# An encoder layer on one core: the squares of the attention heads' outputs, summed in float32r halves instead of float32

## The chip, the core and the metric

The kernel runs on one core of a Trainium2 chip. Its time is the device time of one execution in microseconds (us). Before the change three runs gave 1216.11, 1216.69 and 1217.87 us, so the median is 1216.69 us. The profiled execution took 1216.07 us, and its span, from the first recorded instruction to the last, is 1214.2 us.

## What is computed

Two inputs x of 1024 x 1024 float32 (called g = 0 and g = 1) go through one encoder layer with shared weights. Cut to what matters here:

```
proj = layer_norm(x) @ w_in                 # 3584 columns
o    = (softmax(q1 k1) - lam * softmax(q2 k2)) @ v        # 4 heads, 128 wide
o_da = rms_norm(o, subln_g) * (1 - lam_init) * silu(g_da) # rms over the 128 columns of a head
o_cv = b * conv3(c * h) * silu(g_cv)
o_mx = memory_attention(q_mx, mem) * silu(g_mx)           # 256 memory tokens
y    = layer_norm(ALPHA * x + concat(o_da, o_cv, o_mx) @ w_o)

rms_norm(x, g) = x * rsqrt(mean(square(x)) + 1e-5) * g
```

The change touches the mean of squares inside `rms_norm` alone.

## The kernel before

Everything that feeds a large matrix product is kept as two float32r numbers, a high half and a low half whose sum is the float32 value. A product is then three float32r passes (high x high, high x low, low x high). The helper `hi_of` makes a high half on GpSimd (POOL), and `lo_of` makes the low half by a subtraction, on VectorE (DVE) unless another engine is named. In the profile all of these stand on the helpers' lines, L157 for `hi_of` and L160 for `lo_of`.

The program is a list of jobs: for each input and each of its 4 attention heads (and one memory attention) two halves of 512 query rows. There are thus 16 attention head halves, called head 1 to head 16 below in order of time (the four heads of g = 0 with two halves each, then those of g = 1). A job computes scores (`score`, L678), softmax (L685 the row maximum on DVE, L686 the exponential on ScalarE, ACT), the difference of the two softmaxes (L694 on DVE), transposes of the result on TensorE (PE, `turn`, L736), halves of these (`th` on ACT, `tl` on DVE) and products with v (`av`, L764 to L766, into `po`). Between these steps stand "fillers", eight steps of three 512-column passes for one 128 x 512 tile of the projections (L435 to L437), and at the end the passes of the output projection (L927).

No scheduler reorders anything: the order on each engine is the order in which the program emits instructions. A planner, `Flow`, counts modelled nanoseconds of PE work. `after(ns, fn)` emits `fn` once the count has gone on by `ns`, and `extra` is a list of short PE jobs, each with a due count, of which `run_extra` emits one when it is due, between two filler steps. Every engine works through its queue in order, so an instruction that waits holds all that stand behind it.

At the end of a head half, `end_head` squares `po` on ACT into `sq` (L788), scales `po` by gain and gate on DVE into `og` (L790), and puts `rms` on the `extra` list with a due count 5000 later. `rms` sums the squares over the 128 partitions: each of four 128 x 128 blocks of `sq` is the stationary operand and a column of ones the moving one (L796), so the sums come out with one query row per partition. They go to DVE (`ms`, L798), four small steps on POOL (L800 to L803), a transpose (L810), and by way of memory into `og` (L822).

Small intermediate tiles share a pool of five 128 x 512 buffers, called `ev`; a new tile takes a free buffer and its first writer waits for the last user of the old tile.

Of the kernel before, what the change touches and what calls it, by code (L numbers as in the profile page):

```python
# [27 lines left out]
F32 = mybir.dt.float32  # L28
F32R = mybir.dt.float32r
# [6 lines left out]
P = 128  # L36
D = 1024
S = 1024
HS = 512
# [60 lines left out]
class Flow:  # L100
# [10 lines left out]
    def after(self, ns, fn):  # L111

        done = []

        def once():
            if not done:
                done.append(True)
                fn()
        self.n += 1
        heapq.heappush(self.due, (self.t + ns, self.n, once))  # L120
        return once
# [8 lines left out]
def encoder(ctx, tc, x0, x1, xt1, memt, wt, wo, cols, lam4, rope, ln_rows, y0, y1):  # L130
# [3 lines left out]
    after = fl.after  # L134

    ctx.enter_context(tc.manual_schedule())
    pool = ctx.enter_context(tc.tile_pool(name="sb", bufs=1))
# [8 lines left out]
    def sb(shape, dt, tag, name):  # L146
        return pool.tile(shape, dt, tag=tag, name=name, bufs=BUFS.get(tag, 1))

    def bank(shape, name):

        return psX.tile(shape, F32, tag="x", name=name)

    dma = nc.sync.dma_start
    V, G, A, T = nc.vector, nc.gpsimd, nc.scalar, nc.tensor

    def hi_of(out, x, scale=1.0):
        G.tensor_scalar(out, x, scale, 1.0, op0=ALU.mult, op1=ALU.mult)  # L157

    def lo_of(out, x, hi, eng=None):
        (eng or V).tensor_tensor(out, x, hi.bitcast(F32), op=ALU.subtract)  # L160

    def flat(t, offset, ap):
        return bass.AP(tensor=t.tensor, offset=t.offset + offset, ap=ap)


    const = {}

    def constants():
        ident = const["ident"] = pool.tile([P, P], F32, name="ident")
        make_identity(nc, ident)  # L170
        ones = const["ones"] = pool.tile([P, 1], F32, name="ones")
        G.memset(ones, 1.0)
        mhalf = const["mhalf"] = pool.tile([P, 8], F32, name="mhalf")
        G.memset(mhalf, -0.5)
        ccol = const["ccol"] = pool.tile([P, 32], F32, name="ccol")
        dma(ccol, cols)
        lamt = const["lamt"] = sb([P, 4, DH], F32, "gt", "lamt")
        dma(lamt, flat(lam4, 0, [[0, P], [DH, 4], [1, DH]]))
        const["rope"] = pool.tile([P, 2, S], F32, name="ropet")
# [281 lines left out]
    def store(dst, src, ns=1500):  # L461
        after(ns, lambda: dma(dst, src))
# [165 lines left out]
    class Job:  # L628
# [156 lines left out]
        def end_head(self):  # L785
            po = self.po
            self.sq = sb([P, HS], F32, "sq", "sq")
            A.activation(self.sq, po, AF.Square)  # L788
            self.og = sb([P, HS], F32, "og", "og")
            V.scalar_tensor_tensor(self.og, po, const["gain"], self.gt[0], op0=ALU.mult, op1=ALU.mult)  # L790
            extra.append((fl.t + 5000, self.rms))

        def rms(self):
            pr = bank([P, 4], "pr")
            for i in range(4):
                T.matmul(pr[:, i:i + 1], self.sq[:, i * P:(i + 1) * P], const["ones"], start=True, stop=True)  # L796
            ms, r0 = sb([P, 4], F32, "small", "ms"), self.r0
            V.scalar_tensor_tensor(ms, pr, 1.0 / P, r0, op0=ALU.mult, op1=ALU.mult)  # L798
            rs = sb([P, 4], F32, "small", "rs")
            G.tensor_tensor(ms, ms, r0, op=ALU.mult)  # L800
            G.tensor_scalar(ms, ms, 1.0, EPS, op0=ALU.mult, op1=ALU.add)
            G.tensor_tensor(ms, ms, const["mhalf"][:, 0:4], op=ALU.pow)
            G.tensor_tensor(rs, ms, r0, op=ALU.mult)  # L803
            g, h, half, og = self.g, self.h, self.half, self.og
            rd = dram.tile([4, P], F32, name=f"rd{g}_{h}_{half}")

            def rows():

                pw = bank([4, P], "pw")
                T.transpose(pw, rs, const["ident"])  # L810
                rw = sb([4, P], F32, "sq", "rw")
                V.tensor_copy(rw, pw)
                fl.pe(110)
                after(2500, lambda: dma(rd, rw))
                after(9000, lambda: spread())

                def spread():
                    self.rb = sb([P, HS], F32, "sq", "rb")
                    dma(self.rb, flat(rd, 0, [[0, P], [1, HS]]))

                def fin():
                    G.tensor_tensor(og, og, self.rb, op=ALU.mult)  # L822
                    store(mix_d[g][half][h], og)
                after(13500, fin)
            extra.append((fl.t + 6000, rows))
            fl.pe(100)
# [204 lines left out]
    weights_load(("MV", 0))  # L1031
    load_x(0)
    constants()
    load_x(1)
    for kb in range(KB):
# [84 lines left out]
```

## Time and profile before

| | busy us | share of the span | instructions |
|---|---|---|---|
| PE, matmuls | 1175.9 | 97% | 5881 |
| PE, weight loads (PEld) | 922.0 | 76% | 5881 |
| DVE | 803.0 | 66% | 1156 |
| ACT | 426.2 | 35% | 703 |
| POOL | 415.7 | 34% | 466 |

The profiled execution took 1216.07 us with a span of 1214.2 us, so 1.9 us lie outside the span. Weight loads overlap matmuls, and the end of a matmul is modelled, so the busy share of PE says that it nearly always has work, not that it runs at its peak. The pitch of PE, the time between the starts of two matmuls that follow each other, is the better measure of what one costs. The start times below are microseconds from the start of the span.

### The profile page before, as it was taken

How to read it: one execution, taken by the hardware profiler on the slowest of the kernel's cores; microseconds unless marked ns; L12 is line 12 of the kernel's file. 1: busy time of each engine (PE TensorE's matmuls, PEld its weight loads, DVE VectorE, ACT ScalarE, POOL GpSimd, SP SyncE). 2: the span in 40 equal slices, each digit the busy share in tenths (PEclk: the TensorE clock that was granted, in tenths of full speed). 3: DMA queues.
4: the chain of work that ended last, by engine and by line, in shares of the span. 5: the costliest groups of instructions: out<-in, count | busy, mean ns of one | idle time of the engine just before them, and what ended most of it. 6: DMA issues, size and time to landing. Idle time of an engine off the chain costs nothing.

```text
span 1214.2 us, 15653 instructions
## 1 busy us (share of the span) xinstructions
PE 1175.9 (97%) x5881; PEld 922.0 (76%) x5881; DVE 803.0 (66%) x1156; ACT 426.2 (35%) x703; POOL 415.7 (34%) x466
## 2 busy tenths in 40 slices
PE   8899999999999999999999999999999998899997
PEld 6677777777777777788777777777777877788885
DVE  4779857666677675543766765665655456887776
ACT  4624333334233334334344333433433344111220
POOL 4754423352234430322311113023110346445443
PEclk9999999999999999999999999999999999999999
DMA  8366336433644389753321212312322368354341
GB/s 325 102 230 217 145 130 208 153 144 113 216 156 156 122 281 309 260 191 128 133 71 64 92 40 95 100 68 92 111 78 74 127 222 294 99 196 144 133 145 52
DMA packets 83644, 182.61 MB, mean 150 GB/s; under 512 B 7713, under 2 KB 26353, under 8 KB 83441
## 3 DMA queue, kind: packets, MB, share of 16 engines
q1 hardware_dynamic: 80112, 175.33, 41.3%
q10 hardware_dynamic: 3456, 6.29, 1.3%
q8 instruction: 46, 0.75, 0.3%
q14 instruction: 30, 0.24, 0.1%
HBM read 119.69 MB, written 61.91 MB: 150 GB/s over the span
## 4 chain that ended last, share of the span: by engine, by line
PE 75%; DVE 11%; POOL 3%; issue 3%; ACT 3%; DMA 3%; SPq 0%; POOLq 0%; DVEq 0%; ACTq 0%
PE pout L927 13%; PE ps L678 7%; PE pt L736 5%; PE po L764 3%; PE pG L435 2%; PE po L766 2%; PE po L765 2%; PE pG L437 2%; PE pG L436 2%; DVE mx L685 2%; PE pQ L435 2%; PE pQ L437 2%; PE pQ L436 2%; ACT e L686 2%; PE pV L435 2%
## 5 line engine op out<-in xcount | busy, mean ns | idle before, releaser
L686 ACT ACTIVATE e<-ps,mx 128x1024 f32<-128x1024 f32 x128 | 142.8, 1116 | 295.8 <-DVE mx L685 295.6
L685 DVE TENSOR_REDUCE mx<-ps 128x1 f32<-128x1024 f32 x128 | 150.6, 1218 | 87.7 <-PE ps L678 87.7
L160 DVE TENSOR_TENSOR tl<-pt,th 128x1024 fp32r<-128x1024 f32 x80 | 97.3, 1217 | 11.7 <-ACT th L742 11.6
L927 PE MATMUL pout<-woh,mixh 128*128 128x512 f32 x256 | 100.6, 393 | 0.0
L927 PE MATMUL pout<-woh,mixl 128*128 128x512 f32 x256 | 100.4, 392 | 0.0
L927 PE MATMUL pout<-wol,mixh 128*128 128x512 f32 x256 | 100.2, 391 | 0.0
L742 ACT ACTIVATE th<-pt 128x1024 fp32r<-128x1024 f32 x80 | 82.3, 1029 | 42.6 <-PE pt L736 42.1
L694 DVE SCALAR_TENSOR_TENSOR e<-e,ssum,e 128x1024 f32<-128x1024 f32 x64 | 87.9, 1373 | 0.0
L919 POOL TENSOR_TENSOR xr<-xr,lnrow 128x512 f32<-128x512 f32 x32 | 55.7, 1758 | 68.9 <-DVE xr L916 68.8
L476 POOL TENSOR_TENSOR sw<-sw,ropet 128x512 f32<-128x512 f32 x32 | 41.7, 1302 | 90.7 <-DVE sw L470 88.1
L736 PE MATMUL pt<-ident,e 128*128 128x128 f32 x512 | 66.8, 274 | 4.8 <-ACT e L686 4.8
L736 PEld LDWEIGHTS pt<-ident,e 128*128 128x128 f32 x512 | 58.9, 141 | 16.1 <-ACT e L686 8.1
L678 PE MATMUL ps<-kh,qh 64*128 64x512 f32 x256 | 62.8, 444 | 5.4 <-DVE tl L160 5.4
L722 POOL TENSOR_SCALAR em<-em,rm 128x256 f32<-128x256 f32 x64 | 31.9, 517 | 83.2 <-DVE rm L720 76.4
L160 DVE TENSOR_TENSOR wl<-wraw,wh 128x1024 fp32r<-128x1024 f32 (+1 forms) x33 | 43.0, 1303 | 23.7 <-POOL wh L157 13.8
L908 ACT ACTIVATE mixh<-mraw 128x1024 fp32r<-128x1024 f32 x16 | 17.0, 1061 | 114.6 <-PE pout L927 97.6
L764 PE MATMUL po<-th,vh 128*128 128x512 f32 x128 | 56.7, 443 | 0.0
L927 PEld LDWEIGHTS pout<-woh,mixl 128*128 128x128 f32 x256 | 48.3, 189 | 10.8 <-DVE mixl L160 0.6
L678 PE MATMUL ps<-kl,qh 64*128 64x512 f32 x256 | 54.6, 392 | 1.6 <-DVE kl L479 1.5
L927 PEld LDWEIGHTS pout<-wol,mixh 128*128 128x128 f32 x256 | 48.4, 189 | 10.0
L927 PEld LDWEIGHTS pout<-woh,mixh 128*128 128x128 f32 x256 | 48.4, 189 | 9.9
L678 PE MATMUL ps<-kh,ql 64*128 64x512 f32 x256 | 53.9, 390 | 0.0
(284 smaller groups left out, 3069.9 us busy)
## 6 DMA issues: line engine op xcount, KB each, us to landing
wp<-w SPq DMA_DIRECT2D x80, 512.0 KB, 4.3
wraw<-in_wt SPq DMA_DIRECT2D x32, 512.0 KB, 4.4
w<-wh SPq DMA_DIRECT2D x28, 512.0 KB, 5.4
w<-wl SPq DMA_DIRECT2D x28, 512.0 KB, 3.8
mraw<-mix SPq DMA_DIRECT2D x16, 512.0 KB
xr<-in_x SPq DMA_DIRECT2D x16, 512.0 KB, 6.5
out<-xr ACTq DMA_DIRECT2D x24, 256.0 KB, 2.1
x<-in_x SPq DMA_DIRECT2D x8, 512.0 KB, 4.4
```

Of the source, the lines that this page charges most:

```text
L160: (eng or V).tensor_tensor(out, x, hi.bitcast(F32), op=ALU.subtract)
L435: T.matmul(ps, wh[:, k], hh, start=kb == 0, stop=False)
L436: T.matmul(ps, wh[:, k], hl, start=False, stop=False)
L678: T.matmul(ps[c][:, n], q[r, qt * P:(qt + 1) * P], k[r, n], start=i == 0, stop=i == 2)
L685: V.tensor_reduce(mx[:, c:c + 1], ps[c], AX.X, ALU.max, negate=True)
L686: A.activation(e[c], ps[c], AF.Exp, bias=mx[:, c:c + 1], accum_out=sm[:, c:c + 1])
L694: V.scalar_tensor_tensor(e[0], e[1], st, e[0], op0=ALU.mult, op1=ALU.add)
L736: T.transpose(pt[:, u * HS + i * P:u * HS + (i + 1) * P], self.tiles[i][:, (b + u) * P:(b + u + 1) * P], const["ident"])
L742: A.activation(th, pt, AF.Copy)
L764: T.matmul(self.po, vh[:, k, :], th[:, c], start=k == 0, stop=False)
L919: after(2200 + 2000 * n, lambda c=c: G.tensor_tensor(xt[:, c], xt[:, c], ab[:, c], op=ALU.add))
L927: T.matmul(self.ps, a[:, kb, :], b, start=kb == 0 and ti == 0, stop=kb == KB - 1 and ti == 2)
```

## The change

`sq` is no longer the stationary operand itself. After `end_head` POOL makes its high half `sqh` (a `hi_of`, emitted 1500 later by the planner's count) and DVE its low half `sql` (a `lo_of`, 2700 later). `rms` then does two float32r passes for each of the four blocks, one with the block of `sqh` and one with that of `sql` as stationary operand, added up in PSUM. The column of ones becomes two columns, in float32r, and the sums are read from every second column. `sqh` and `sql` take two of the five `ev` buffers until `rms` has run.

```diff
-        ones = const["ones"] = pool.tile([P, 1], F32, name="ones")
-        G.memset(ones, 1.0)
+        ones = const["ones"] = pool.tile([P, 2], F32R, name="ones")
+        onef = pool.tile([P, 2], F32, name="onef")
+        G.memset(onef, 1.0)
+        hi_of(ones, onef)
...
             V.scalar_tensor_tensor(self.og, po, const["gain"], self.gt[0], op0=ALU.mult, op1=ALU.mult)
+            self.sh, self.sl = [sb([P, HS], F32R, "ev", n) for n in ("sqh", "sql")]
+            after(1500, lambda: hi_of(self.sh, self.sq))
+
+            after(2700, lambda: lo_of(self.sl, self.sq, self.sh))
             extra.append((fl.t + 5000, self.rms))
 
         def rms(self):
-            pr = bank([P, 4], "pr")
+            pw = bank([P, 4, 2], "pr")
             for i in range(4):
-                T.matmul(pr[:, i:i + 1], self.sq[:, i * P:(i + 1) * P], const["ones"], start=True, stop=True)
+                for n, s in enumerate((self.sh, self.sl)):
+                    T.matmul(pw[:, i], s[:, i * P:(i + 1) * P], const["ones"], start=n == 0, stop=n == 1)
+            pr = pw[:, :, 0]
```

The order of the instructions stays as it was on every engine, apart from what is added. On PE, at head 1, before (pG is a filler tile, hTh and hTl are the halves of the normalised input, wh and wl those of a weight tile):

```order
L437 MATMUL pG<-hTh_0_181,wl 128x512
L796 MATMUL pr<-ones,sq 128x1 x4
L435 MATMUL pG<-hTh_0_183,wh 128x512
L436 MATMUL pG<-hTl_0_184,wh 128x512
L437 MATMUL pG<-hTh_0_183,wl 128x512
```

The same place on PE in the changed kernel, where the lines have moved down by two to eight:

```order
L439 MATMUL pG<-hTh_0_183,wl 128x512
L803 MATMUL pr<-ones,sqh 128x2
L803 MATMUL pr<-ones,sql 128x2
L803 MATMUL pr<-ones,sqh 128x2
L803 MATMUL pr<-ones,sql 128x2
L803 MATMUL pr<-ones,sqh 128x2
L803 MATMUL pr<-ones,sql 128x2
L803 MATMUL pr<-ones,sqh 128x2
L803 MATMUL pr<-ones,sql 128x2
L437 MATMUL pG<-hTh_0_185,wh 128x512
```

Four float32 matmuls became eight float32r ones at the same place between two filler steps, and the second of them already needs `sql`. On DVE, at head 1, in the changed kernel (wl is the low half of a weight tile, e the softmax of one head, xt a tile of the second input's normalisation; before, the row of `sql` is missing and the rest is the same):

```order
L160 TENSOR_TENSOR wl<-wraw,wh 128x1024
L693 RECIPROCAL r<-sm 128x2
L694 TENSOR_SCALAR ssum<-sm,r,lamneg 128x1
L695 COPY r_1647<-r 128x1
L696 SCALAR_TENSOR_TENSOR e_1650<-e_1651,ssum,e_1650 128x1024
L160 TENSOR_TENSOR sql<-sq,sqh 128x512
L300 SCALAR_TENSOR_TENSOR xt<-xt,ccol,strow 128x512
L160 TENSOR_TENSOR tl<-pt,th 128x1024
L806 SCALAR_TENSOR_TENSOR ms<-pr,r_1647 128x4
```

`sql` stands behind the weight split and the softmax difference, and in front of `xt`. On POOL, at head 7, whose next job is a memory attention (em is its softmax, which POOL scales in eight pieces; vmst the halves of its v), in the changed kernel:

```order
L830 TENSOR_TENSOR og<-og,rb 128x512
L157 TENSOR_SCALAR vmst<-vmraw 128x8x64
L724 TENSOR_SCALAR em<-em,rm 128x256 x3
L157 TENSOR_SCALAR sqh<-sq 128x512
L724 TENSOR_SCALAR em<-em,rm 128x256 x5
L808 TENSOR_TENSOR ms<-ms,r_3690 128x4
```

Before, the eight pieces of `em` follow each other; now `sqh` stands behind the third of them.

## Rows read from the trace of the kernel before

**Rows 1.** The page, chain that ended last: share of the span by engine.
```profile
PE 75%; DVE 11%; POOL 3%; issue 3%; ACT 3%; DMA 3%; SPq 0%; POOLq 0%; DVEq 0%; ACTq 0%
```
**Rows 2.** Timeline of PE, head 1: start us, us, engine line op out<-in, shape, xcount.
```profile
172.41 0.39 PE L437 MATMUL pG<-hTh,wl 128*128 128x512 f32 x1
172.64 0.95 PE L796 MATMUL pr<-ones,sq 128*128 128x1 f32 x8
...
173.77 0.39 PE L436 MATMUL pG<-hTl,wh 128*128 128x512 f32 x1
```
**Rows 3.** Timeline of the weight loads, head 1.
```profile
173.31 0.19 PEld L796 LDWEIGHTS pr<-ones,sq 128*128 128x128 f32 x1
173.42 0.19 PEld L435 LDWEIGHTS pG<-hTh,wh 128*128 128x128 f32 x1
173.53 0.19 PEld L436 LDWEIGHTS pG<-hTl,wh 128*128 128x128 f32 x1
```
**Rows 4.** The chain that ended last, 975 to 1060 us: start us, us, what.
```profile
975.69 1.62 PE ps L708 x23
```
**Rows 5.** Timelines of POOL (head 1) and DVE (head 3).
```profile
175.44 0.62 POOL L157 TENSOR_SCALAR hhi<-xt 128x512 fp32r<-128x512 f32 x1
...
290.89 0.69 DVE L160 TENSOR_TENSOR vl<-vt,vh 128x512 fp32r<-128x512 f32 x1
```
**Rows 6.** Timeline of DVE, head 1.
```profile
173.16 0.75 DVE L298 SCALAR_TENSOR_TENSOR xt<-xt,ccol,strow 128x512 f32<-128x512 f32 x1
```
**Rows 7.** Timelines of DVE and PE, head 5.
```profile
407.10 0.74 DVE L298 SCALAR_TENSOR_TENSOR xt<-xt,ccol,strow 128x512 f32<-128x512 f32 x1
...
405.98 0.95 PE L796 MATMUL pr<-ones,sq 128*128 128x1 f32 x8
```
**Rows 8.** Timelines of DVE and PE, head 4.
```profile
342.59 0.75 DVE L298 SCALAR_TENSOR_TENSOR xt<-xt,ccol,strow 128x512 f32<-128x512 f32 x1
...
340.75 0.95 PE L796 MATMUL pr<-ones,sq 128*128 128x1 f32 x8
```
**Rows 9.** Timelines of DVE and PE, head 6 and head 14.
```profile
464.02 1.22 DVE L160 TENSOR_TENSOR tl<-pt,th 128x1024 fp32r<-128x1024 f32 x1
...
464.64 0.95 PE L796 MATMUL pr<-ones,sq 128*128 128x1 f32 x8
...
902.44 1.22 DVE L160 TENSOR_TENSOR tl<-pt,th 128x1024 fp32r<-128x1024 f32 x1
...
903.06 0.95 PE L796 MATMUL pr<-ones,sq 128*128 128x1 f32 x8
```
**Rows 10.** Timelines of POOL and PE, head 7.
```profile
508.89 3.66 POOL L722 TENSOR_SCALAR em<-em,rm 128x256 f32<-128x256 f32 x8 [19.47 <-DVE rm L720]
...
510.02 0.95 PE L796 MATMUL pr<-ones,sq 128*128 128x1 f32 x8
```
**Rows 11.** Timelines of POOL, DVE and PE, head 16.
```profile
984.53 3.18 POOL L722 TENSOR_SCALAR em<-em,rm 128x256 f32<-128x256 f32 x6
...
985.47 1.21 DVE L160 TENSOR_TENSOR tl<-pt,th 128x1024 fp32r<-128x1024 f32 x1
...
984.63 0.95 PE L796 MATMUL pr<-ones,sq 128*128 128x1 f32 x8
...
986.74 0.50 PE L760 MATMUL po<-tl,vmst 128*128 128x512 f32 x1
```
**Rows 12.** Waits of the weight loads, 150 to 1000 us, then 985 to 1056: us, times, longest.
```profile
PEld ps L678 <- DVE tl L160: 6.9, 7, 1.3
...
PEld pt L736 <- ACT e L686: 6.8, 9, 2.0
...
PEld po L760 <- DVE tl L160: 9.1, 5, 4.4
```
**Rows 13.** The chain that ended last, 165 to 300 us.
```profile
246.35 0.24 PE pQ L437
246.63 0.73 DVE sw L470 x2
```

## The prediction

> **What bounds the kernel now.** I read the chain that ended last first: 75% of the span is PE, and DVE is next with 11% [rows 1]. Then the timeline of PE around the changed step. Filler passes follow each other there without a gap, and the four float32 matmuls of `rms` stand among them as eight passes, each with its own weight load [rows 2]. The reader is to see that nothing on PE waits at this place: whatever is put there, work or a wait, moves all that follows. Last I read the timelines of DVE and POOL at the same times, for where the two new instructions would fall.
>
> **What the passes cost.** From the L437 at 172.41 to the L436 at 173.77 are 1.36 us [rows 2]. In the same distance two filler passes would have taken 0.47 at the pitch of 0.23 that the rows show (172.41 to 172.64), so the eight passes of `rms` cost 0.89 us, or 0.112 each. The loads give the same pitch: 0.11 from the last load of `sq` to the first of the filler [rows 3]. It is the load of 128 columns that paces them, not one column of ones.
>
> The changed kernel has eight passes again, each with a load of 128 columns, now float32r, and two columns of ones. The trace has no float32r pass that short. The nearest rows are the float32r loads that follow: 0.19 us long like the float32 ones, and 0.11 apart from 173.42 to 173.53 [rows 3]. I take 0.112 for a pass: nothing gained, nothing lost. From below, the 64-row score passes go at 0.07 each (23 in 1.62 us, [rows 4]); that would save 8 x 0.042 = 0.34 us per head half, 5.4 in all. From above, a filler pass of 512 columns takes 0.23; that would add 8 x 0.12 = 0.96 per head half, 15 in all, but it is set by 512 columns, and two are far from that.
>
> The Trainium skill, "TensorE: Matmul & The Clock Gate", section "Weight-path perf modes", says that a load of 128 weights whose type isn't FP32 is made by a faster way, about twice as fast as measured there. If float32r counts as such, eight passes would cost about half of 0.89, an estimate by that page, and the change would give back some 7 us over 16 heads. This trace doesn't bear it out: float32r and float32 loads are both 0.19 long and 0.11 apart [rows 3].
>
> **What is added beside.** A `hi_of` of 128 x 512 takes 0.62 us on POOL, a `lo_of` 0.69 on DVE [rows 5]: 16 x 0.62 = 10 us of POOL, 16 x 0.69 = 11 us of DVE. Both engines have room on average, so as work they cost nothing. The memset and the `hi_of` of the ones at the start are hidden by the loads of the first weights, and would be a few tenths if they weren't. The two `ev` buffers are each free before they are needed by the order; I count nothing for them.
>
> **The wait that is added.** Before, the passes needed `sq` alone, which ACT had finished before PE came. Now the first pass needs `sqh` and the second `sql`, and PE works in order: behind the second pass stand the other six, the fillers and the next scores. `sql` stands on DVE behind what the planner put there before it. So the sum is, for each head, the end of `sql`, plus what passes from the end of a DVE instruction to the PE matmul that waited for it, minus the time at which PE now starts the passes. That passing-on is 0.06: `tl` ends at 985.47 + 1.21 = 986.68, and the L760 that waits for it starts at 986.74 [rows 11].
>
> - Head 1: `sql` takes the place of `xt`, which starts at 173.16 [rows 6], and ends at 173.85. PE gets there at 172.64 [rows 2]. The wait is 173.85 + 0.06 - 172.64 = 1.3 us. I take `sqh` as done by then, since POOL has no work of length between `sq` and the `xt` that it adds later. Heads 2, 3 and 5 look the same, a weight split (L160, 1024 wide) and the softmax difference ahead of `sql` on DVE. The last of them, head 5: 407.10 + 0.69 + 0.06 - 405.98 = 1.9 [rows 7]; heads 2 and 3 give 1.2 and 1.9 in the same way.
> - Head 4 has a step of the convolution in front of `sql` as well: 342.59 + 0.75 - 340.75 = 2.6 [rows 8]. So heads 1 to 5 make 1.3 + 1.2 + 1.9 + 2.6 + 1.9 = 8.9.
> - Heads 6 and 9 to 14 have no weight split at this place, since their weights come ready split from memory. `sql` takes the place of `tl` (in two of them of a `vl`): 464.02 + 0.75 - 464.64 = 0.1 for the first and 902.44 + 0.75 - 903.06 = 0.1 for the last [rows 9]. Of the seven four give 0.1 and three 0.4, in all 1.6.
> - Heads 7, 8 and 15 have a memory attention around them. POOL starts the eight pieces of `em` at 508.89 and takes 0.46 for each [rows 10]; three of them end at 510.26, `sqh` at 510.88, `sql` at 511.57. PE is there at 510.02 [rows 10]: 1.6. Head 8 gives 1.6 and head 15 1.9 in the same way, in all 5.1. Here the `tl` of this stretch stands behind `sql` on DVE and comes later too, but PE, itself late, needs it only after the fillers that follow the passes.
> - Head 16: two more pieces of `em` after 984.53 at 0.53 each, then `sqh` to 986.21 and `sql` to 986.90; PE is there at 984.63 [rows 11], so 2.3 + 0.06 = 2.4. `tl` goes 1.4 later, but PE comes to its L760 later still.
>
> The sum: 8.9 + 1.6 + 5.1 + 2.4 = 18.0 us of waiting on PE, passes 0. Nothing makes it up beside: the stretches between heads are chains of PE passes, and where the chain leaves PE it starts again from a PE step, as the shuffle at 246.63 from the filler that ends just before [rows 13]; so it moves with PE. The instructions behind `sql` on DVE move by 0.6 us, and PE, which moves by more in most heads, doesn't see it. The profiled execution took 1216.07 us, 0.6 less than the median of the runs. On its own time the sum is 1216.07 + 18.0 = 1234.1 us, and that is the forecast.
>
> **Rivals.**
>
> - The passes are cheaper. With 0.07 for a pass the sum is 18.0 - 5.4 = 12.6, that is 1228.7 us; with half the cost of each it is 18.0 - 7.1 = 10.9, that is 1227. For it speaks that float32r matmuls are the ones the kernel prefers everywhere; against it the equal pitch of the loads [rows 3].
> - The lateness is given back, and the kernel is no slower. PE has waits of its own further on: 6.9 us for `tl` and 6.8 for exponentials between 150 and 1000 us, 9.1 for `tl` in the stretch from 985 to 1056 [rows 12], together 22.8. If what PE waits for there runs by its own clock (DMAs, POOL, the split weights) and not after PE, a PE that comes 18.0 late waits that much less, and the time stays at about 1216. It decides at the point where these waits are longer than the lateness that PE brings with it; the last stretch alone could take 9.1, which leaves 1216.1 + 8.9 = 1225. Against it: `tl` and the exponentials themselves begin with scores and transposes that PE makes.
> - The waits are longer. `sql` and the work behind it on DVE come later than in the rows of before, because DVE, POOL and PE have also been moved by the heads before; if each of the nine long waits grows by 0.7, one more instruction of 128 x 512 in front, the sum is 18.0 + 6.3 = 24.3, that is 1240.4.
> - That the change does nothing: the short waits (1.6) and nothing else would make 1217.7. That would need `sql` to be early in the nine long cases, and the order puts it behind the split weights and the pieces of `em`.
>
> **How the numbers follow.** The forecast has 0.66, with a range of its own of 1230 to 1238. Cheaper passes have 0.12 (1227 to 1229), given back 0.10 (half of it wholly, half to about 1225), longer waits 0.11 (to 1241), nothing 0.01. The range 1222 to 1241 leaves out the wholly given back, the do-nothing case and the tails on either side, the far upper bound of the passes among them, and holds some 0.85. About 0.2%, some 2.4 us, is what a measurement of this kernel can tell from no change. Slower by more has 0.93, within it 0.05, faster 0.02, for which cheaper passes and lateness given back would have to come together.
>
> **What would show it.** In the profile after, PE or its loads should wait for `sql` (on `lo_of`'s line) 16 times, and for `sqh` some times, 18 us in all, most of it at heads 1 to 5, 7, 8, 15 and 16, with next to none at 6 and 9 to 14. The passes on `sqh` and `sql` should number 128, again 0.11 us apart after the wait. DVE should be busy about 814 us, POOL about 426. The starts of the later jobs should lag by the sum of the waits so far: 8.9 us after head 5, some 15.6 at head 16. The prediction is wrong if the passes come 0.07 apart or less, if the waits are there but the lag shrinks between heads, or if `sql` is ready before PE is.

## The result

| | before | after |
|---|---|---|
| median of the runs, us | 1216.87 (1216.11 to 1217.87, 4 runs) | 1244.72 (1244.2 to 1245.89, 4 runs) |
| profiled execution, us | 1216.07 | 1244.74 |
| span, us | 1214.2 | 1243.0 |
| mean granted clock of TensorE | 0.996 | 0.985 |

The changed kernel is slower: the ratio is 1.023, with a 95% interval of 1.0214 to 1.0246, or 27.9 us between the medians. The forecast was 18 us. By the page, against the table of the kernel before, PE is busy 13.8 us longer, DVE 10.4 and POOL 10.4:

```profile
PE 1189.7 (96%) x5881; PEld 932.3 (75%) x5881; DVE 813.4 (65%) x1172; ACT 426.6 (34%) x703; POOL 426.1 (34%) x483
```

PE has as many instructions as before. So more busy time means that single ones have become longer; time in which PE stands still isn't busy. That is the first hint that waits are not the whole of it; the granted clock, 0.985 for 0.996, is the second.

**The waits are there.** The first two rows are waits of the matmuls, the next two those of the weight loads, over the whole span (us in all, how often, the longest):

```profile
PE pr L803 <- DVE sql L160: 11.7, 11, 2.4
PE pr L803 <- POOL sqh L157: 4.8, 4, 1.8
...
PEld pr L803 <- DVE sql L160: 14.4, 16, 2.6
PEld pr L803 <- POOL sqh L157: 6.6, 4, 2.2
```

The forecast had 18.0 us; the trace has 16.5 at the matmuls and 21.0 at the loads, which become idle a little before the matmuls do. The loads wait for `sql` 16 times, once per head half. At head 1 it is as the working has it, `sql` on DVE (first row) and the passes on PE:

```profile
173.28 0.69 DVE L160 TENSOR_TENSOR sql<-sq,sqh 128x512 fp32r<-128x512 f32 x1
...
172.74 0.17 PE L803 MATMUL pr<-ones,sqh 128*128 128x2 f32 x1
174.02 0.27 PE L803 MATMUL pr<-ones,sql 128*128 128x2 f32 x1 [1.11 <-DVE sql L160]
174.15 0.25 PE L803 MATMUL pr<-ones,sqh 128*128 128x2 f32 x1
```

The rows that answer to [rows 2] are the last two: after the wait a pass follows 0.13 behind, the later ones 0.11 to 0.12, as before. `sql` starts 0.12 later than `xt` did [rows 6] and PE comes 0.10 later; the wait of 1.28 between the first two passes less the usual 0.11 is 1.2, forecast 1.3.

**The clock is not as before.** At head 3 PE waits 1.81 us, and the clock falls while the passes that follow run. First the PE timeline, then windows of PE alone (from:to, us, PE busy and matmuls, granted clock, DMA share, GB/s):

```profile
293.69 0.27 PE L803 MATMUL pr<-ones,sql 128*128 128x2 f32 x1 [1.81 <-DVE sql L160]
293.82 0.25 PE L803 MATMUL pr<-ones,sqh 128*128 128x2 f32 x1
293.93 0.31 PE L803 MATMUL pr<-ones,sql 128*128 128x2 f32 x1
294.10 0.35 PE L803 MATMUL pr<-ones,sqh 128*128 128x2 f32 x1
294.31 0.35 PE L803 MATMUL pr<-ones,sql 128*128 128x2 f32 x1
...
295.53 0.63 PE L438 MATMUL pG<-hTl,wh 128*128 128x512 f32 x1
295.95 0.63 PE L439 MATMUL pG<-hTh,wl 128*128 128x512 f32 x1
```
```profile
291.00:295.00 4.00, 2.19 (x13) 0.87 0.32 131
295.00:299.00 4.00, 4.00 (x11) 0.50 0.01 4
299.00:303.00 4.00, 4.00 (x18) 0.77 0.69 249
```

The pitch of the passes of `rms` goes from 0.11 to 0.21, that of the fillers from 0.23 to 0.43 (295.53 to 295.95). A clock of 0.50 is the 1.2 GHz level, 1.00 is 2.4 GHz. Before, the same place ran at full clock, with twice as many matmuls in four microseconds:

```profile
293.00:297.00 4.00, 4.00 (x23) 1.00 0.51 186
```

The same happens behind heads 4, 5, 7 and 15 (middle rows) and behind 8 (0.71 from 575 to 579), but not behind heads 1 and 2 (first row) and not behind head 16 (last row):

```profile
176.00:180.00 4.00, 4.00 (x23) 1.00 0.52 193
...
352.00:356.00 4.00, 4.00 (x12) 0.57 0.29 107
421.00:425.00 4.00, 4.00 (x13) 0.66 0.17 66
529.00:533.00 4.00, 4.00 (x13) 0.57 1.02 387
974.00:978.00 4.00, 4.00 (x11) 0.50 0.05 21
...
1016.00:1020.00 4.00, 4.00 (x23) 1.00 0.30 83
```

**Where the 28.8 us of span stand.** The best ruler is the start of each head's `sq` on ACT in both traces, after minus before. For head 4 (before, then after) it is 344.70 - 337.14 = 7.56 us:

```profile
337.14 0.59 ACT L788 ACTIVATE sq<-po 128x512 f32<-128x512 f32 x1
```
```profile
344.70 0.59 ACT L790 ACTIVATE sq<-po 128x512 f32<-128x512 f32 x1
```

The growth of this lag from one head to the next is what a head's `rms` cost in the end. The last column is the same for experiment `e5_wait_filled`, below.

| head | wait forecast, us | lag added, changed kernel | lag added, e5 |
|---|---|---|---|
| 1, 2 | 1.3, 1.2 | 1.3, 1.2 | 1.3, 1.2 |
| 3 | 1.9 | 4.9 | 1.9 |
| 4 | 2.6 | 4.1 | 2.6 |
| 5 | 1.9 | 3.6 | 2.0 |
| 6 | 0.1 | 0.1 | 0.1 |
| 7 | 1.6 | 3.2 | 1.6 |
| 8 | 1.6 | 3.0 | 1.7 |
| 9 to 14 | 1.5 | 0.2 | 0.9 |
| 15 | 1.9 | 5.7 | 2.6 |
| 16 and the end | 2.4 | 1.2 | 2.6 |

Heads 3, 4, 5, 7, 8 and 15 cost 12.1 us more than in e5, and the rest 2.0 less, 1.4 of it in the last stretch.

### The profile page after: what moved, and what is told of

Same layout as the page of the kernel before. It is cut to its first block, busy times and chain, and to the rows that moved or that the text cites. A ratio compares the mean times of both kernels' runs of the same rounds, so it can differ in the third digit from the quotient of the medians.

```text
span 1243.0 us, 15698 instructions
## 1 busy us (share of the span) xinstructions
PE 1189.7 (96%) x5881; PEld 932.3 (75%) x5881; DVE 813.4 (65%) x1172; ACT 426.6 (34%) x703; POOL 426.1 (34%) x483
## 5 line engine op out<-in xcount | busy, mean ns | idle before, releaser
L935 PEld LDWEIGHTS pout<-woh,mixl 128*128 128x128 f32 x256 | 48.3, 189 | 10.8 <-DVE mixl L160 0.6
```

Source lines behind the costliest of these rows:

```text
L935: T.matmul(self.ps, a[:, kb, :], b, start=kb == 0 and ti == 0, stop=kb == KB - 1 and ti == 2)
```

## The experiments

All are compared with the kernel before on the same chip (medians 1216.2 to 1216.5). Where letters stand in an expectation, W is the theory that the waits for `sqh` and `sql` make the loss, C that the granted clock behind them adds to it, K the rival of C, and T that `tl` stands held behind `sql`.

**e1: `rms` later.** If PE comes to `rms` when `sql` has long been made, the waits are gone, and all else of the change stays.

```diff
-            extra.append((fl.t + 5000, self.rms))
+            extra.append((fl.t + 8500, self.rms))
```

> The changed kernel with the passes of rms due 8500 instead of 5000 after the end of a head, so that sqh and sql are ready before PE comes; nothing else changed. Theory W (the 28 us are about 18 us of PE waiting for sqh and sql, plus some 10 us of PE at its lower clock behind the longer of these waits): both go, no wait on sql over 0.2 us, mean granted clock back to 0.995, 1216 to 1219 us. Theory L (the added POOL and DVE work and the two buffers cost it): 1235 us or more, since all of that work is still there. Theory P (float32r passes of two columns cost more than float32 ones): 1240 us or more.

Measured: 1227.34 us (1224.55 to 1230.38), ratio 1.0099 (1.008 to 1.0117). The profiled run took 1224.55 us at a mean clock of 0.996; over the four runs the time goes up to 1230.38 as the mean clock goes down to 0.987. What follows is of the profiled run, so it accounts for 8.6 us of span and not for the 11 between the medians. No wait for `sqh` or `sql` is left, and up to the start of head 15's `sq` the lag is only 1.2 us. So what the passes cost isn't it. But 3.4 us come between heads 15 and 16 and 4 behind head 16, which I had not expected. On DVE at head 15 `sql` waits 1.79 us for POOL and holds `tl` (first two rows, with a step of the convolution between them), and PE waits for `tl` in place of `sql` (third row). The clock does not fall behind this wait, though it is longer than any that `rms` has in the changed kernel (last row, a window of PE):

```profile
951.09 0.96 DVE L160 TENSOR_TENSOR sql<-sq,sqh 128x512 fp32r<-128x512 f32 x1 [1.79 <-POOL sqh L157]
...
952.86 1.21 DVE L160 TENSOR_TENSOR tl<-pt,th 128x1024 fp32r<-128x1024 f32 x1
...
954.12 0.50 PE L768 MATMUL po<-tl,vh 128*128 128x512 f32 x1 [3.37 <-DVE tl L160]
...
952.00:956.00 4.00, 1.88 (x8) 1.00 0.12 47
```

**e2: the halves at once.** Both are emitted right behind `og`, so nothing is queued ahead of them that was emitted later.

```diff
-            after(1500, lambda: hi_of(self.sh, self.sq))
-
-            after(2700, lambda: lo_of(self.sl, self.sq, self.sh))
+            hi_of(self.sh, self.sq)
+            lo_of(self.sl, self.sq, self.sh)
```

> The changed kernel with hi_of and lo_of of the squares emitted at once at the end of a head, instead of 1500 and 2700 later; the passes stay due at 5000. sql then stands right behind og on DVE, ahead of the weight splits, and sqh ahead of most of the memory softmax on POOL. Theory W: sql ends some 1.3 us after sq, before PE comes at 3 us, so no wait on PE and no low clock; DVE gives 0.7 us per head earlier than now, which PE need not see: 1216 to 1221 us. Theories L and P: 1235 us or more.

Measured: 1216.63 us (10 runs, 1215.43 to 1217.79), ratio 1.0002 (0.9992 to 1.0011). The change's whole work, made in another place, costs nothing that can be measured. DVE is as loaded as in the changed kernel:

```profile
PE 1174.4 (97%) x5881; PEld 922.6 (76%) x5881; DVE 817.0 (67%) x1172; ACT 426.2 (35%) x703; POOL 425.8 (35%) x483
```

The loss is thus one of order, not of the load on DVE and POOL.

**e3: the halves made, but not used.** `rms` is as before, on `sq`; what is left of the change is the work on DVE and POOL, in the changed kernel's places.

```diff
...
-                for n, s in enumerate((self.sh, self.sl)):
-                    T.matmul(pw[:, i], s[:, i * P:(i + 1) * P], const["ones"], start=n == 0, stop=n == 1)
+                T.matmul(pr[:, i:i + 1], self.sq[:, i * P:(i + 1) * P], const["onef"], start=True, stop=True)
```

> The halves of the squares are made as in the changed kernel, at the same places on POOL and DVE, but rms goes back to four float32 matmuls on sq, as before: PE doesn't wait for the halves. Theory W: within 1.5 us of the kernel before, 1216 to 1218.5 us. Theory L: most of the 28 us stay, 1235 us or more. Theory P: 1216 to 1219 us as well.

Measured: 1220.84 us (1219.09 to 1221.2), ratio 1.0033 (1.002 to 1.0046), some 2 us over what was expected. Between heads 15 and 16 the lag grows by 4.2. Again PE waits for `tl` there, and again the clock falls: the fillers behind it take 0.63 us by the trace for the 0.39 to 0.40 of full clock.

```profile
950.90 0.50 PE L768 MATMUL po<-tl,vh 128*128 128x512 f32 x1 [2.48 <-DVE tl L160]
...
952.06 0.63 PE L437 MATMUL pGM<-hTh,wp 128*128 128x512 f32 x1
```
```profile
948.00:952.00 4.00, 1.52 (x6) 0.97 0.00 0
952.00:956.00 4.00, 4.00 (x16) 0.60 0.47 131
```

Here no pass of `rms` stands at the wait: those ended 4 us earlier, at full clock, with five passes of 512 columns between. For the clock to fall behind a wait the halves are not needed at it. The two prices can be read apart at this one matmul: in e1 it waits 3.37 us, the clock stays at 1.00 and the lag grows by 3.4; here it waits 2.48, the clock falls and the lag grows by 4.2.

**e4: both passes on the same block.** ACT writes `sq` as float32r, both passes of each block read it, and the sum is halved; the low half of the squares is left out, and so are the two instructions that make the halves. No half is made and nothing is waited for, but the passes are 128 as in the changed kernel.

```diff
-            self.sq = sb([P, HS], F32, "sq", "sq")
+            self.sq = sb([P, HS], F32R, "sq", "sq")
...
-                for n, s in enumerate((self.sh, self.sl)):
+                for n, s in enumerate((self.sq, self.sq)):
...
-            V.scalar_tensor_tensor(ms, pr, 1.0 / P, r0, op0=ALU.mult, op1=ALU.mult)
+            V.scalar_tensor_tensor(ms, pr, 0.5 / P, r0, op0=ALU.mult, op1=ALU.mult)
```

> No halves: ACT writes the squares as float32r, and rms makes eight float32r passes of two columns on them, each block twice (the sum is halved). It leaves out the low half of the squares. The price of the passes alone, with nothing to wait for. Theory W with passes at 0.112 us as I took them: 1215.5 to 1218.5 us, passes 0.11 apart. Passes at half cost: 1210 us. Theory P: 1225 us or more.

Measured: 1215.17 us (10 runs, 1214.38 to 1216.38), ratio 0.9992 (0.9982 to 1.0001). The loads (first row; min, median, max ns) and the pitch are those of float32: eight passes from 171.66 to 172.47, 0.81 us, as before from 172.64 to 173.45.

```profile
L799 PEld LDWEIGHTS pr<-ones,sq x128: 187/192/192, 171.4 to 982.4; 128*128 128x128 f32 x128
...
171.66 0.95 PE L799 MATMUL pr<-ones,sq 128*128 128x2 f32 x8
172.47 0.48 PE L437 MATMUL pG<-hTh,wh 128*128 128x512 f32 x1
```

**e5: the wait filled.** This tells the clock from the waits. Ahead of `rms` PE gets useless passes of 512 columns, as many as fit into the forecast wait at a pitch of 0.23 (at heads 15 and 16 eight, which leaves a wait of 0.7 for `sql`). `sql` is no earlier, but PE works until it comes.

```diff
...
-            pw = bank([P, 4, 2], "pr")
+            pw = bank([P, HS], "pr")
+            head = 8 * self.g + 2 * self.h + self.half + 1
+            for n in range({1: 5, 2: 5, 3: 8, 4: 11, 5: 8, 7: 7, 8: 7, 15: 8, 16: 8}.get(head, 0)):
+                T.matmul(pw.rearrange("p (i c) -> p i c", c=P), const["busy"], const["busy"][:, None, :].to_broadcast([P, 4, P]), start=True, stop=True)
+            pw = pw[:, 0:8].rearrange("p (i c) -> p i c", c=2)
```

> The changed kernel with useless passes of 512 columns put in front of rms at the nine heads with a long wait (5 to 11 of them, as many as fill the wait that I had worked out), so that PE works while sqh and sql come. PE starts the next filler no earlier than in the changed kernel. Theory C (of the 28 us some 10 or more are the lower clock that follows the long waits): the granted clock stays at 1.00 behind heads 3, 4, 5, 7, 8 and 15, and the time falls by 9 to 13 us, to 1232 to 1236 us. Theory K (the part beyond the 18 us of waits is knock-on of DVE and POOL, and the low clock only goes with it): no gain, 1243 us or more.

Measured: 1233.9 us (1232.9 to 1234.91), ratio 1.0141 (1.0124 to 1.0158). It does more than the changed kernel and is 10.8 us faster. At head 3 the useless passes end where `sql` is ready (its first pass starts at 293.73, in the changed kernel at 293.69), and behind them the fillers keep their 0.39 and the clock its 1.00. So it is at the other heads up to 15: from 100 to 1000 us the granted clock is 1.00.

```profile
291.77 2.00 PE L807 MATMUL pr<-busy 128*128 128x512 f32 x8
...
293.73 0.27 PE L811 MATMUL pr<-ones,sql 128*128 128x2 f32 x1
...
294.85 0.39 PE L442 MATMUL pG<-hTl,wh 128*128 128x512 f32 x1
```
```profile
295.00:299.00 4.00, 4.00 (x20) 1.00 0.14 52
```

**e6: a third of the way.** The due count goes from 5000 to 6000, which shortens the waits without removing them.

```diff
-            extra.append((fl.t + 5000, self.rms))
+            extra.append((fl.t + 6000, self.rms))
```

> The changed kernel with rms due at 6000 instead of 5000, some 1.1 us of PE work later: each wait gets shorter by that, those of heads 1 and 2 nearly vanish, those of heads 3, 5, 7, 8 and 15 shrink to 0.5 to 0.8 us, head 4 to 1.5. Theory C: with shorter waits the clock isn't lowered behind most heads; what stays is some 6 us of waits, the low clock behind one or two heads, and the memory stretches at heads 15 and 16: 1224 to 1230 us. Theory K: the time falls by the waits alone, 9 us, to 1235 us or more.

Measured: 1232.68 us (1231.34 to 1235.04), ratio 1.0135 (1.0119 to 1.0152), clock 0.988: between the 1224 to 1230 that C expected and the 1235 of its rival, so by itself it decides nothing. The waits fell to 7.9 us, more than by half. But the clock falls all the same behind head 4, after a wait of 1.72 (first row, and the window behind it), behind head 8, after one of 0.72 (third and fourth row), and behind head 16. So 16.5 of the 28 us stay with less than half of the waits.

```profile
344.51 0.27 PE L803 MATMUL pr<-ones,sql 128*128 128x2 f32 x1 [1.72 <-DVE sql L160]
...
348.00:360.00 12.00, 12.00 (x59) 0.92 0.40 132
...
560.33 0.27 PE L803 MATMUL pr<-ones,sql 128*128 128x2 f32 x1 [0.72 <-DVE sql L160]
...
560.00:564.00 4.00, 3.67 (x15) 0.70 0.17 66
```

**e7: one pass.** ACT writes `sq` as float32r, and four passes read it; the low half of the squares is left out, so the sums are those of squares rounded to float32r.

```diff
...
-                for n, s in enumerate((self.sh, self.sl)):
-                    T.matmul(pw[:, i], s[:, i * P:(i + 1) * P], const["ones"], start=n == 0, stop=n == 1)
+                T.matmul(pw[:, i], self.sq[:, i * P:(i + 1) * P], const["ones"], start=True, stop=True)
```

> ACT writes the squares as float32r and rms makes four float32r passes on them, without a low half. It leaves out the low half of the squares. Against the run with each block twice it takes away 64 passes; at 0.112 us each that is 7.2 us: 1207 to 1210 us. If the passes were hidden behind the weight loads of other work or PE weren't the bound, 1214 us or more.

Measured: 1209.83 us (1209.46 to 1210.0), ratio 0.9945 (0.993 to 0.996). It is the only version that beats both kernels. Against e4 it is (0.9992 - 0.9945) x 1216.3 = 5.7 us faster for 64 passes fewer, 0.09 for each, near the 0.112 of the forecast.

**e8: `rms` later, and the halves at once in the last attention head alone.** If in e1 it was `sql` that held `tl`, moving it at heads 15 and 16 should take most of the rest away.

```diff
-            after(1500, lambda: hi_of(self.sh, self.sq))
-
-            after(2700, lambda: lo_of(self.sl, self.sq, self.sh))
-            extra.append((fl.t + 5000, self.rms))
+            now = self.g == 1 and self.h == 3
+            for ns, fn in ((1500, lambda: hi_of(self.sh, self.sq)), (2700, lambda: lo_of(self.sl, self.sq, self.sh))):
+                fn() if now else after(ns, fn)
+            extra.append((fl.t + 8500, self.rms))
```

> The kernel with rms due 8500 later (e1_rms_later), and at its last two head halves, 15 and 16, sqh and sql emitted at once. It asks where the 11 us of e1_rms_later are. Theory T (sql, which waits on DVE for sqh and so for three pieces of the memory softmax on POOL, holds the tl behind it, and PE waits for that): the 3.4 us between heads 15 and 16 and most of the 4 us behind head 16 go, 1217 to 1221 us. Theory S (sums that come 3500 later are late for the output projection by themselves): 1224 us or more.

Measured: 1220.06 us (10 runs, 1218.01 to 1221.88), ratio 1.0026 (1.0017 to 1.0036). Of e1's 11 us between the medians 7 are gone; between the two profiled runs, at mean clocks of 0.996 and 0.995, it is 3.9 (spans of 1222.8 and 1218.9). The wait at the same matmul is 1.20 for 3.37, and the lag grows by 1.2 there:

```profile
952.83 0.50 PE L768 MATMUL po<-tl,vh 128*128 128x512 f32 x1 [1.20 <-DVE tl L160]
```

## Why the prediction was wrong

**The waits: right.** Who waits, for whom and at which heads came out as worked out. In e5 the lag grows by the forecast wait to within 0.2 us at each of heads 1 to 8. Head 15 takes 0.7 more, and the changed kernel's trace shows where it comes from: three pieces of `em` take 2.36 us there (before, all eight took 5.06, which is 1.9 for three), and `sql` takes 0.95 in place of 0.69. Heads 9 to 14 take 0.9 in place of 1.5. (Head 16 was added up 0.1 too high: 2.27 + 0.06 is 2.3.) The sum of 18.0 is 18.7 in the span of e5, and the time of that kernel, 1233.9, is the 1234.1 of the forecast; that it is so close is in part luck, as the last stretch shows below. "The starts of the later jobs should lag by the sum of the waits so far: 8.9 us after head 5, some 15.6 at head 16" holds for e5 (9.2 and 16.1), not for the changed kernel (15.2 and 27.6). None of the three signs by which the prediction was to be known as wrong came: the passes are 0.11 apart, `sql` is late, and the lag grows where the third sign had it shrink.

**The passes: right.** e4 has them without the rest and stands at 0.9992 of the kernel before. The loads of float32r are 0.19 long and 0.11 apart, as [rows 3] had it. The faster load, by which the rival of cheaper passes would have saved some 7 us, is not seen in any run here.

**DVE and POOL: right as load, wrong in one place as order.** e2 carries the added 16 x 0.69 and 16 x 0.62 at no cost. But "the `tl` of this stretch stands behind `sql` on DVE and comes later too, but PE, itself late, needs it only after the fillers" holds only while PE is late: where PE is not (e3, e1) it waits for that `tl`, 2.5 and 3.4 us, and e8 takes most of it away. In the changed kernel it stays hidden, as forecast: that matmul has no wait for `tl` in its trace.

**The step that failed** is the sum: "8.9 + 1.6 + 5.1 + 2.4 = 18.0 us of waiting on PE, passes 0. Nothing makes it up beside". It counted the time that PE stands still and took it that PE goes on afterwards at the pitch of [rows 2], and does not mention the clock behind a wait: that term stands at nothing, without a reason. PE doesn't go on so. Behind six of the nine long waits PE runs at the 1.2 GHz level for some microseconds, where fillers stand 0.43 apart in place of 0.23. By the windows this costs 3.4 us at head 3 ((0.13 + 0.50 + 0.23) x 4) and 1.7 at head 4 (0.43 x 4); by the table it is 12.1 us at six heads. Against e5 the last stretch takes 1.4 off that, since e5 loses more to the clock there:

```profile
1010.00:1040.00 30.00, 23.90 (x127) 0.97 0.63 211
1040.00:1090.00 50.00, 46.93 (x213) 0.95 0.55 182
```
```profile
1000.00:1030.00 30.00, 25.24 (x129) 0.92 0.67 220
1030.00:1080.00 50.00, 46.77 (x211) 0.95 0.54 176
```

The upper rows are of the changed kernel, 0.9 + 2.5 = 3.4 us lost to the clock, the lower of e5, 2.4 + 2.5 = 4.9. The missed term as a whole is 1243.0 - 1232.9 = 10.1 us between the spans, 1244.72 - 1233.9 = 10.8 between the medians. That it is the clock is shown by e5: `sql` is as late as in the changed kernel, but with PE at work until then the clock stays at 1.00, and the time is the forecast.

The trace of the kernel before could have told it. Its ten waits of 0.9 to 1.5 us between 60 and 980 us left the clock at 1.00, but the two longest in the last stretch, 3.98 and 2.41 us, are followed by low ones. The first of them, with the window behind it:

```profile
1008.88 0.50 PE L760 MATMUL po<-tl,vmst 128*128 128x512 f32 x1 [3.98 <-DVE tl L160]
...
1008.00:1012.00 4.00, 3.12 (x10) 0.76 1.07 381
```

The rival of longer waits came nearest (1240.4), by chance and with the wrong cause: with PE at full clock (e5) the lag comes to 18.7, not 24.3. Lateness is not given back from one head to the next, where the lag shrinks by 0.2 us at most in the changed kernel and in e5. In the last stretch a little is: the changed kernel's lag grows by 1.2 there after waits of 1.77 + 0.72, while that first wait for `tl` falls from 3.98 to 3.24 and one for `em` from 0.94 to 0.37. So "nothing makes it up beside" was wrong by 1.3 us. In e5 this is hidden, since its clock loses more there (4.9 us, against 50 x 0.07 = 3.5 in the kernel before, from 1010 to 1060 us). That the 2.6 of e5 in the last row of the table agrees with the forecast is luck.

**What stays open** is why the clock fell behind heads 3, 4, 5, 7, 8 and 15 and not behind 16. Heads 1 and 2 had shorter waits (1.1 us at the matmul), but at head 7 there are two of 0.7 with one pass between, and the clock falls, while at head 16 there are 1.8 and 0.7 in the same form, and it doesn't:

```profile
526.30 0.27 PE L803 MATMUL pr<-ones,sqh 128*128 128x2 f32 x1 [0.74 <-POOL sqh L157]
527.29 0.27 PE L803 MATMUL pr<-ones,sql 128*128 128x2 f32 x1 [0.72 <-DVE sql L160]
```
```profile
1014.11 0.27 PE L803 MATMUL pr<-ones,sqh 128*128 128x2 f32 x1 [1.77 <-POOL sqh L157]
1015.10 0.27 PE L803 MATMUL pr<-ones,sql 128*128 128x2 f32 x1 [0.72 <-DVE sql L160]
```

The other runs say the same: the clock fell behind 0.72 us at head 8 of e6 and stayed at 1.00 behind 3.37 in e1. So the length of the wait alone does not decide it. What else does was not tried.

## What to carry to other kernels

On a PE that is the bound, a new wait can cost twice: the time it stands still, and then a stretch at half clock that may follow, here 1.4 to 3.1 us for each wait that had one. Look at the granted clock behind the waits that the kernel already has, and put both ends into the range. When an operand gets a new producer on an in-order engine, look at what that producer stands behind, and at what stands behind it: the same halves cost 28 us in one place of the queue and nothing a few instructions earlier, and a producer that must wait holds work (here `tl`) that has nothing to do with it.

## What the runs showed of the hardware

- TensorE's granted clock went from 1.00 to 0.50 after waits of 0.7 us (e6, head 8) to 2.5 us (e3 at 950.90) in an otherwise full stretch, with and without short passes at the wait, and came back some microseconds later. It stayed at 1.00 after 2.5 us in two pieces (head 16 of the changed kernel) and after 3.4 us (e1 at 954.12). Filling the wait with passes whose result nobody reads made the kernel 10.8 us faster.
- The pace of weight loads follows the clock as that of the fillers does: at head 3 the passes of `rms`, which are paced by their loads, went from 0.11 to 0.21 apart, and the loads themselves from 0.19 us to 0.33.
- A float32 matmul of one column with a 128 x 128 stationary block and two float32r passes of two columns take the same time, 0.81 us for four blocks in both (from the first pass to the filler behind). Halving the passes (e7) saved 0.09 us for each one dropped.
